# Expert inputs by indirect DMA and transposes in place of one-hot products, with gates applied per slot

## The chip, the cores and the metric

The kernel runs on one core of a Trainium2 chip. The metric is the device time of one execution in microseconds (us); lower is better. Engines are named as the profile names them: PE (TensorE, with PEld for its weight loads), DVE (VectorE), ACT (ScalarE), POOL (GpSimd) and SP (SyncE, which issues the weight loads).

## The reference, cut to what matters

The model has two layers over 512 tokens of 1024 channels. Each layer is a token mixer followed by a mixture of 16 experts, of which each token takes two. All arithmetic is float32.

```python
def grouped_moe(x, router_w, router_b, w1, w3, w2):
    logits = xt @ router_w + router_b
    scores = softmax(logits)
    ...                                   # best of 4 expert groups, then its top 2 experts
    gates = top_w / sum(top_w)
    def expert_block(args):               # rows of the tokens that chose expert e
        xb, e = args
        hb = silu(xb @ w1[e]) * (xb @ w3[e])
        return hb @ w2[e]
    ys = ys * buf_gate[:, None]
    out = segment_sum(ys, buf_tok)        # back to the tokens

h = layer_norm(ALPHA * h + y, ln1_g[l], ln1_b[l])
y = grouped_moe(h, router_w, router_b, moe_w1[l], moe_w3[l], moe_w2[l])
h = layer_norm(ALPHA * h + y, ln2_g[l], ln2_b[l])
```

## The kernel before, in words

A float32 product is made of three passes in a rounded format (`mm3`, L341): each operand is split into a high part (ACT's cast, L337) and a low part (DVE's subtraction, L338), and PE adds high x high, high x low and low x high (L343, L345, L344). Weights come from DRAM in pieces of 1 MB on SP's queue (`load`, L323) into a ring of ten buffers; each piece is split as two halves of 128x1024.

`moe` (L1281) is the stage that the change touches; it runs once in each layer. `route` (L1069) chooses experts and gives each token its rank within its expert (`rke`). Each expert has 96 slots (`CAP`). Experts are taken in groups (`GROUPS`: 0-1, 2-4, 5-7, 8-10, 11-13, 14-15). For a group, `one_hot` (L1185) builds on DVE a matrix `A` of zeros and ones (tokens x slots), and `gather_x` (L1201) multiplies the stored rows by it on PE: for each of 8 channel blocks, the high rows `hi` and the low rows `lo` times `A`, over 4 blocks of tokens, 64 products for a group, 288 columns wide for a group of three experts and 256 for a group of two (L1212). `gathered` (L1216) copies the results from PSUM to the `hx` tiles, high parts on ACT (L1221), low parts on DVE (L1222). The first group is gathered apart, while the last block of tokens is still being normed (L1323).

The loop over `e` (L1330) issues, for each expert: the first product with W1 (48 matmuls), the product with W2 of the expert before (48, `expert_out`, L1260), a share of the gathering for the next group, the product with W3 (48), and `expert_mid` (L1250): silu (ACT, L1256), the product of both halves (DVE, L1257), and a transposition on PE (`transpose_split`, L1224, matmul line L1231) that ACT (L1233) and DVE (L1234) take out of PSUM as high and low parts. `expert_out` copies its result out on ACT (L1278) and writes it to DRAM (`yd`). In iteration 1, `places` (L1122), some fifty small DVE operations, works out where each token finds its two results, and the gates. In iteration 14 `rest` (L1401) transposes `A` of experts 14 and 15, whose results never go to DRAM, and `overflow` (L1452) tests whether any expert has more than 96 tokens; every engine meets at that test.

At the end `collect` (L1418) fetches for each block of tokens the two result rows by indirect DMA from POOL's queue (L1425), scales the first by its gate on ACT (L1429), and adds the second times its gate on DVE (L1433). `combine` (L1502) adds everything in PSUM and norms it.

While layer 0's experts run, POOL also works out the parameters of the next layer's state-space mixer (`s5_params`). Before the experts, `settle` (L1051) norms the rows of each block of tokens and splits them into `hi` and `lo`. The order of the work on each engine is set ahead by a planner, from program order, priorities and the few hints `issue_after`; on the chip each engine then runs its list in order.

Of the kernel before, what the change touches and what calls it, by code (L numbers as in the profile page):

```python
# [19 lines left out]
P = 128  # L20
T = 512
# [12 lines left out]
WIDE = 3 * CAP * 4  # L34
# [25 lines left out]
def shape_constants():  # L60
    c = {}
    p = np.arange(P)
    ident = np.eye(P, dtype=np.float32)
    shut = np.where(p[None, :] >= p[:, None], -1e30, 0.0).astype(np.float32)
    before = (p[:, None] < p[None, :]).astype(np.float32)
    iota = np.broadcast_to(p.astype(np.float32) + 1.0, (P, P))
    misc = np.zeros((P, 64), np.float32)
    misc[:, 0:16] = np.arange(16)
    misc[:, 16:32] = 16 - np.arange(16)
    misc[:, 32:36] = 4 - np.arange(4)  # L70
    misc[:, 36] = -0.5
    misc[:, 37] = 1.0
    misc[:, 40:40 + len(TURNS)] = TURNS
    c["shut"] = np.concatenate([shut, before], 1)
# [45 lines left out]
class Kernel:  # L120
# [8 lines left out]
    def run(self):  # L129
# [7 lines left out]
        self.y_dram = self.dram.tile([(NG + SPILL) * CAP, D], F32, name="yd")  # L137
# [115 lines left out]
    def hx(self, n):  # L253
        return self.keep.tile([P, WIDE], F32R, tag="hx", name="hx", bufs=8)[:, 0:n]
# [696 lines left out]
    def row_loads(self, l):  # L951
# [19 lines left out]
        if l == 0:  # L971
            zr = self.mr.tile([P, 2048], F32, tag="raw", name="zr", bufs=2)[0:CAP, 0:D]
            nc.gpsimd.memset(zr, 0.0)
        yield
# [146 lines left out]

    def places(self, r, pool):  # L1122
        V = self.nc.vector
        t = lambda nm, sh, dt=F32: pool.tile([P] + sh, dt, tag=nm, name=nm, bufs=1)
        ps, M, s = r["ps"], r["M"], r["s"]
        oh, v, wm = t("oh", [128]), t("v", [2, NT]), t("wm", [NT])
# [7 lines left out]
        for j in range(2):  # L1134
            V.tensor_tensor(rk[j], oh[:, j], s, OP.mult)
            V.tensor_reduce(v[:, j], rk[j], AX.X, OP.add)
        gt, den = t("gt", [2, NT]), t("den", [NT])
        V.tensor_tensor(den, v[:, 0], v[:, 1], OP.add)
        V.reciprocal(den, den)
        V.tensor_tensor(gt, v, den[:, None, :].to_broadcast([P, 2, NT]), OP.mult)  # L1140
# [27 lines left out]
        pf, gm0, gl = t("pf", [2, NT]), t("gm0", [2, NT]), t("gl", [2, NT])  # L1168
# [5 lines left out]
        V.tensor_scalar(gm0, gt, float(1.0 / ALPHA), None, OP.mult)  # L1174
        V.tensor_tensor(b2, b2, gm0, OP.mult)
        last = t("glast", [2, NT])
        for x in range(2):
            V.tensor_tensor(gl, b2, oh[:, :, :, NG + x], OP.mult)
            V.tensor_tensor(last[:, x], gl[:, 0], gl[:, 1], OP.add)
            V.tensor_tensor(gm0, gm0, gl, OP.subtract)  # L1180
        V.tensor_scalar(b2, gm0, 0.0, None, OP.is_gt)
        V.tensor_tensor(pos, pf, b2, OP.mult)
        r.update(gm=gm0, pos=pos, exi=exi, mci=mci, cnti=cnti, last=last)

    def one_hot(self, pool, r, group, parts=1):  # L1185
        e, n = group
        w = self.width(n)
# [10 lines left out]
    def width(self, n):  # L1198
        return CAP if n == 3 else P

    def gather_x(self, A, out, ks):  # L1201
        nc = self.nc
        n, w = A.shape[2:]
        for k in ks:
            if n == 3:
                ps = [self.bank(t, "gx")[:, 0:n * w] for t in ("zo", "zz")[k % 2]]
            else:
                b = self.bank("oz"[k % 2], "gx")
                ps = [b[:, 0:n * w], b[:, n * w:]]
            for s, rows in enumerate((self.xh, self.rl)):  # L1210
                for c in range(NT):
                    nc.tensor.matmul(ps[s], rows[c][:, k * P:(k + 1) * P], A[:, c].rearrange("p e s -> p (e s)"),  # L1212
                                     start=c == 0, stop=c == NT - 1)
            self.gathered(ps, out, k, n, w)

# [8 lines left out]
    def transpose_split(self, src, h, lo, tags="oz"):  # L1224
        nc = self.nc
        w = src.shape[0]
        for half in range(2):
            ps = self.bank(tags[half], "tx")[:, 0:4 * w]
            for q in range(4):
# [3 lines left out]
            self.mid = (nc.scalar.copy(h[:, sl], ps).ins,  # L1233
                        nc.vector.tensor_tensor(lo[:, sl], ps, h[:, sl].bitcast(F32), OP.subtract).ins)  # L1234
# [25 lines left out]
    def expert_out(self, pool, w, g, mkload, dst, us=range(4), ps=None, y=None):  # L1260
# [15 lines left out]
        for n in range(2):  # L1276
            ns = slice(n * 512, (n + 1) * 512)
            nc.scalar.copy(y[0:CAP, ns], ps[n])  # L1278
        nc.scalar.dma_start(dst, y[0:CAP])

    def moe(self, l, lg, nb, rs):  # L1281
# [6 lines left out]
        with self.pool("mw") as mw, ExitStack() as spare:  # L1288
# [41 lines left out]
            for e in range(NE):  # L1330
# [6 lines left out]
                at, n = e - GROUPS[g][0], GROUPS[g][1]  # L1337
                if at == 0:
                    cur, nxt = nxt, ([], [])
                w = at * self.width(n)  # L1340
                x = [[t[k // 4][:, k % 4, w:w + CAP] for k in range(KD)] for t in cur]
                with ExitStack() as after:
# [4 lines left out]
                    self.calm = False  # L1347
                if e == NE - 1:
                    half = self.expert_out(mw, W2, pend, mk(e - 1), None, range(2))
                elif pend is not None:  # L1350
                    y13 = self.keep.tile([P, WIDE], F32, tag="hx", name="y", bufs=8)[:, 0:D] if e == NE - 2 else None
                    self.expert_out(mw, W2, pend, mk(e - 1), Y[(e - 1) * CAP:e * CAP, :], y=y13)
                if e < NE - 2:
                    if at == 0:
                        A = self.one_hot(mw, r, GROUPS[g + 1])
                    self.gather_x(A, nxt, range(*((0, 3, 6, 8), (0, 4, 8))[n == 2][at:at + 2]))
# [44 lines left out]
    def rest(self, A, r, mw):  # L1401
# [3 lines left out]
        pg = self.bank("z", "gs")  # L1405
        for x in range(2):
            ps = self.bank("o", "at")
            for c in range(NT):
                nc.tensor.transpose(ps[0:CAP, c * P:(c + 1) * P], A[:, c, x, 0:CAP].bitcast(F32), self.ident)
            nc.scalar.copy(self.at[x], ps[0:CAP])  # L1410
            for c in range(NT):
                nc.tensor.matmul(pg[0:CAP, x:x + 1], A[:, c, x, 0:CAP].bitcast(F32), r["last"][:, x, c:c + 1],
                                 start=c == 0, stop=c == NT - 1)
            gs = self.hi.tile([P, 1], F32, name=f"gs{x}")[0:CAP]
            nc.vector.tensor_copy(gs, pg[0:CAP, x:x + 1])
            self.gs.append(gs)

    def collect(self, r, Y, slots):  # L1418
# [3 lines left out]
        for c in range(NT):  # L1422
# [4 lines left out]
            act, dve = self.cut  # L1427
# [24 lines left out]
    def overflow(self, l, r, mw, Y, wf):  # L1452
# [4 lines left out]
        with tc.If(most > CAP):  # L1457
            A = mw.tile([P, WIDE], F32R, tag="A", name="oA", bufs=1)[:, 0:NT * P].rearrange("p (c s) -> p c s", c=NT)
            sl = mw.tile([P, D], F32, tag="sl", name="osl", bufs=1)
            xh, xl, wt = (self.hx(D) for _ in range(3))  # L1460
            wh, wl = wt[:, 0:T], wt[:, T:]
            rk = self.keep.tile([P, NT], F32, tag="ork", name="ork")
            x = [[t[:, k * P:(k + 1) * P] for k in range(KD)] for t in (xh, xl)]
            for b in range(1, BLOCKS):
                with tc.For_i(0, NE, 1) as e:
                    ce = nc.values_load(r["cnti"][0:1, bass.ds(e, 1)], min_val=0, max_val=T)
                    with tc.If(ce > CAP * b):
# [3 lines left out]
                                        rk[:, :, None].to_broadcast([P, NT, P]), OP.is_equal)  # L1471
                        for k in range(KD):
# [23 lines left out]
                        for n in range(2):  # L1496
                            nc.scalar.copy(sl[:, n * T:(n + 1) * T], product(W2, n))
# [74 lines left out]
```

## Time and profile before

| | us |
|---|---|
| median of 3 runs | 2233.0 (2229.27 to 2236.12) |
| the profiled execution, its own time | 2232.6 |
| its span in the trace | 2230.8 |

| engine | busy, us | share of the span |
|---|---|---|
| PE | 2161.2 | 97% |
| PEld | 1617.5 | 73% |
| DVE | 1554.7 | 70% |
| ACT | 1246.3 | 56% |
| POOL | 437.3 | 20% |

The experts' stage of layer 0 runs from about 505 to 1130 us of the span, that of layer 1 from about 1596 us to the end. A matmul's record lasts longer than the time until the next one starts, since matmuls are pipelined; the cost of one is therefore read as the distance between starts.

### The profile page before, as it was taken

The numbers are of one execution on the slowest core, as the hardware profiler recorded it, in microseconds if no ns is written. First come the engines' busy times: TensorE is split into PE (matmuls) and PEld (weight loads), VectorE is DVE, ScalarE is ACT, GpSimd is POOL, SyncE is SP. The second block draws the span as 40 slices with busy tenths as digits, with TensorE's granted clock in tenths as the row PEclk, the third lists the DMA queues.
The fourth block names the chain that finished last, engine by engine and source line by source line (L and its number), as shares of the span: only waits on it lengthen the run. The fifth ranks groups of instructions, "written<-read, shape, count | busy, mean of one in ns | idle before, by whom it ended". The sixth has DMA issues, their size and how long they took to land. (4 is left out here: it accounts for less than half of the span.)

```text
span 2230.8 us, 28031 instructions
## 1 busy us (share of the span) xinstructions
PE 2161.2 (97%) x10498; PEld 1617.5 (73%) x10501; DVE 1554.7 (70%) x1986; ACT 1246.3 (56%) x1580; POOL 437.3 (20%) x491
## 2 busy tenths in 40 slices
PE   7999999999999999999999999999899999999997
PEld 5678678877777777776676877888677777777765
DVE  8443533458988998887864435334798888888878
ACT  4333123336777777777744322223477777777764
POOL 5310141120039920000250204211300000000003
PEclk9989999999999999999999999999999999999999
DMA  6121275327989999997931313343389999999965
GB/s 193 51 59 45 69 255 191 113 71 281 336 310 351 337 360 355 342 358 281 376 114 38 75 57 128 117 170 130 125 322 355 351 357 351 346 358 360 340 262 197
DMA packets 188171, 517.96 MB, mean 232 GB/s; under 512 B 17968, under 2 KB 71856, under 8 KB 188016
## 3 DMA queue, kind: packets, MB, share of 16 engines
q1 hardware_dynamic: 173312, 476.69, 59.7%
q10 hardware_dynamic: 10960, 25.67, 3.5%
q0 software_dynamic: 3744, 13.63, 1.6%
q8 instruction: 85, 1.39, 0.3%
q14 instruction: 70, 0.57, 0.1%
HBM read 490.13 MB, written 22.81 MB: 230 GB/s over the span
## 5 line engine op out<-in xcount | busy, mean ns | idle before, releaser
L338 DVE TENSOR_TENSOR wl<-raw,wh 128x1024 fp32r<-128x1024 f32 x850 | 1046.1, 1250 | 342.2 <-ACT wh L337 328.6
L337 ACT CAST wh<-raw 128x1024 fp32r<-128x1024 f32 x872 | 907.3, 1051 | 457.9 <-PE e L345 197.8
L344 PE MATMUL e<-wl,hx 128*96 128x512 f32 x1024 | 406.3, 397 | 7.5 <-PEq L1457 6.7
L345 PE MATMUL e<-wh,hx 128*96 128x512 f32 x1024 | 404.0, 395 | 0.0
L343 PE MATMUL e<-wh,hx 128*96 128x512 f32 x1024 | 391.2, 394 | 0.3 <-ACT wh L337 0.3
L343 PE MATMUL pjf<-hx,wh 128*128 128x512 f32 x608 | 245.1, 403 | 4.8 <-DVE v L210 4.8
L345 PE MATMUL pjf<-hx,wl 128*128 128x512 f32 x608 | 244.3, 402 | 2.1 <-DVE wl L338 2.1
L344 PE MATMUL pjf<-hx,wh 128*128 128x512 f32 x608 | 244.9, 403 | 0.8 <-DVE hx L211 0.7
L344 PEld LDWEIGHTS e<-wl,hx 128*96 128x96 f32 x1024 | 165.3, 161 | 75.8 <-DVE wl L338 5.5
L343 PEld LDWEIGHTS e<-wh,hx 128*96 128x96 f32 x1024 | 165.2, 162 | 67.5 <-ACT wh L337 0.7
L345 PEld LDWEIGHTS e<-wh,hx 128*96 128x96 f32 x1024 | 165.9, 162 | 65.8 <-issue 0.5
L344 PE MATMUL e<-wl,gh 128*96 128x512 f32 x512 | 201.3, 393 | 0.2
L345 PE MATMUL e<-wh,gl 128*96 128x512 f32 x512 | 201.3, 393 | 0.0
L1425 POOL DMA_INDIRECT yg<-yd,pos x16 | 28.0, 1751 | 882.0 <-DVE wl L338 586.4
L343 PE MATMUL e<-wh,gh 128*96 128x512 f32 x512 | 195.0, 393 | 0.0
L343 PEld LDWEIGHTS pjf<-hx,wh 128*128 128x128 f32 x608 | 115.6, 190 | 33.9 <-DVE v L210 6.0
L345 PEld LDWEIGHTS pjf<-hx,wl 128*128 128x128 f32 x608 | 115.6, 190 | 29.6 <-DVE wl L338 2.6
L344 PEld LDWEIGHTS pjf<-hx,wh 128*128 128x128 f32 x608 | 115.4, 190 | 29.5 <-DVE hx L211 1.9
L344 PEld LDWEIGHTS e<-wl,gh 128*96 128x96 f32 x512 | 82.7, 161 | 36.3 <-DVE wl L338 2.2
L343 PEld LDWEIGHTS e<-wh,gh 128*96 128x96 f32 x512 | 82.5, 161 | 35.2
L345 PEld LDWEIGHTS e<-wh,gl 128*96 128x96 f32 x512 | 82.5, 161 | 34.3
L1212 PE MATMUL gx<-A,hi 128*128 128x288 f32 (+1 forms) x640 | 97.3, 296 | 0.0
(489 smaller groups left out, 2853.8 us busy)
## 6 DMA issues: line engine op xcount, KB each, us to landing
raw<-in_moe_w_dram SPq DMA_DIRECT2D x384, 1024.0 KB, 6.0
raw<-in_w_in_dram SPq DMA_DIRECT2D x44, 1024.0 KB, 5.2
yd<-y ACTq DMA_DIRECT2D x28, 384.0 KB, 4.8
raw<-in_w_out_dram SPq DMA_DIRECT2D x8, 1024.0 KB, 6.9
yd<-zr ACTq DMA_DIRECT2D x14, 384.0 KB, 6.2
row<-hd POOLq DMA_DIRECT2D x8, 512.0 KB, 7.7
rawu<-in_w_up_c_dram SPq DMA_DIRECT2D x8, 512.0 KB, 3.4
tab<-in_ct_dram ACTq DMA_DIRECT2D x12, 256.0 KB, 2.7
```

The source lines that it names most:

```text
L337: self.cut = (nc.scalar.copy(hv, v).ins, (eng or nc.vector).tensor_tensor(lv, v, hv.bitcast(F32), OP.subtract).ins)
L338: (eng or nc.vector).tensor_tensor(lv, v, hv.bitcast(F32), OP.subtract).ins)
L343: mm(out, lh, rh, start=start, stop=False)
L344: mm(out, lh, rl, start=False, stop=False)
L345: mm(out, ll, rh, start=False, stop=stop)
L1212: nc.tensor.matmul(ps[s], rows[c][:, k * P:(k + 1) * P], A[:, c].rearrange("p e s -> p (e s)"), start=c == 0, stop=c == NT - 1)
L1425: nc.gpsimd.indirect_dma_start(out=yg[j], out_offset=None, in_=Y[:, :], in_offset=bass.IndirectOffsetOnAxis(ap=r["pos"][:, j, c:c + 1], ax ...
```

## The change

`settle` now also writes the normed rows of each block of tokens to a DRAM tensor `x_dram`, from POOL's queue. For experts 2 to 15 (14 of 16), `gather_x` is gone. A new function `slots` builds the one-hot matrix in bfloat16 and multiplies it on PE, for each expert, by a table of only 5 columns (the token's index in two parts, its gate in three), which gives for each slot the row to fetch and its gate. `fetch` then gets the 96 rows of an expert by an indirect DMA from POOL's queue, one expert ahead, and the existing `transpose_split` turns them on PE into channels x slots and splits them. Experts 0 and 1 are gathered as before. `gates`, a new list of small DVE operations in iteration 0, makes the table; `places` loses its operations on gates. `expert_out` scales by the slot's gate as it copies the result out on ACT, so `collect` only adds two rows, the first half of the channels on DVE and the second on POOL. `rest` takes the bfloat16 `A` and no longer computes gates. The `hx` tiles shrink from 1152 to 1024 columns, and one row of zeros at the end of `yd` stands for results that are not in DRAM.

```diff
@@ settle
         self.apply_norm(t, [t[:, 0:512], t[:, 512:1024]], nb, rs, self.gb, adds)
+        nc.gpsimd.dma_start(self.x_dram[c * P:(c + 1) * P, :], t)
@@ new
+    def gates(self, r, pool):
+        ...
+        V.tensor_copy(R[:, :, :, 0], self.misc[:, 56:57, None].to_broadcast([P, NT, NE]))
+        V.tensor_copy(R[:, :, :, 1], self.misc[:, 57:61, None].to_broadcast([P, NT, NE]))
+        V.tensor_tensor(G, r["M"], r["s"], OP.mult)
+        V.tensor_reduce(den, G, AX.X, OP.add)
+        ...
+    def slots(self, pool, r, g):
+        ...
+        A = pool.tile([P, 2 * WIDE], BF16, tag="A", name="As", bufs=1)[:, 0:NT * n * CAP]
+        ...
+        V.tensor_tensor(A, self.iota[:, None, None, 0:CAP].to_broadcast([P, NT, n, CAP]),
+                        r["rke"][:, :, e:e + n, None].to_broadcast([P, NT, n, CAP]), OP.is_equal)
+        ps = self.bank("o", "ix")[0:CAP]
+        for x in range(n):
+            for c in range(NT):
+                nc.tensor.matmul(ps[:, x * COLS:(x + 1) * COLS], A[:, c, x], r["R"][:, c, e + x],
+                                 start=c == 0, stop=c == NT - 1)
+        ...
+        V.tensor_copy(part, p3[:, :, 0])
+        V.tensor_tensor(idx, p3[:, :, 1], part, OP.add)
+        V.tensor_reduce(gate, p3[:, :, 2:], AX.X, OP.add)
+        ...
+    def fetch(self, r, e):
+        t = self.keep.tile([P, D], F32, tag="hx", name="xr", bufs=8)[0:CAP]
+        self.nc.gpsimd.indirect_dma_start(out=t, out_offset=None, in_=self.x_dram[:, :],
+                                          in_offset=bass.IndirectOffsetOnAxis(ap=r["idx"][e], axis=0))
+        return t
@@ expert_out
-            nc.scalar.copy(y[0:CAP, ns], ps[n])
+            nc.scalar.activation(y[0:CAP, ns], ps[n], AF.Copy, scale=gate)
@@ moe, loop over e
+                if 0 < e < NE - 1:
+                    xr = self.fetch(r, e + 1)
                 ...
                     a1 = self.expert_in(W1, x, mk(e), ("pj", "pj"), ready if e == 0 else ())
+                if e == 0:
+                    with tc.issue_after(self.chosen):
+                        self.gates(r, self.hi)
+                        self.slots(mw, r, 0)
                 ...
-                if e < NE - 2:
-                    if at == 0:
-                        A = self.one_hot(mw, r, GROUPS[g + 1])
-                    self.gather_x(A, nxt, range(*((0, 3, 6, 8), (0, 4, 8))[n == 2][at:at + 2]))
+                if at == 0 and e < NE - 2:
+                    A = self.slots(mw, r, g + 1)
+                if 0 < e < NE - 1:
+                    cur = self.transpose_split(xr, self.hx(KD * CAP), self.hx(KD * CAP), "zo", False)
@@ rest
-                nc.tensor.transpose(ps[0:CAP, c * P:(c + 1) * P], A[:, c, x, 0:CAP].bitcast(F32), self.ident)
+                nc.tensor.matmul(ps[0:CAP, c * P:(c + 1) * P], A[:, c, x], self.ident_b, start=True, stop=True)
             ...
-            for c in range(NT):
-                nc.tensor.matmul(pg[0:CAP, x:x + 1], A[:, c, x, 0:CAP].bitcast(F32), r["last"][:, x, c:c + 1],
-                                 start=c == 0, stop=c == NT - 1)
@@ collect
-            with tc.issue_after(act):
-                nc.scalar.activation(yg[0], yg[0], AF.Copy, scale=r["gm"][:, 0, c:c + 1])
-            with tc.issue_after(dve):
-                for i in range(2):
+            with tc.issue_after(self.cut[1]):
+                for i, eng in enumerate((nc.vector, nc.gpsimd)):
                     sl = slice(i * 512, (i + 1) * 512)
-                    nc.vector.scalar_tensor_tensor(yg[0][:, sl], yg[1][:, sl], r["gm"][:, 1, c:c + 1], yg[0][:, sl],
-                                                   OP.mult, OP.add)
+                    eng.tensor_tensor(yg[0][:, sl], yg[1][:, sl], yg[0][:, sl], OP.add)
```

## Rows read from the trace of the kernel before

**Rows 1.** Busy time of each engine by stretch, then clock, DMA share, GB/s.

```profile
530.00:560.00 30.00, 30.00 (x141) 21.30 (x140) 27.26 (x42) 23.03 (x26) 0.00 (x0) 1.00 0.89 316
...
760.00:800.00 40.00, 39.07 (x180) 27.33 (x179) 39.81 (x35) 30.14 (x35) 35.37 (x25) 1.00 0.96 339
...
840.00:880.00 40.00, 40.00 (x193) 28.78 (x191) 34.95 (x35) 30.85 (x37) 0.00 (x0) 1.00 0.97 351
...
1980.00:2020.00 40.00, 40.00 (x186) 28.57 (x185) 36.38 (x35) 31.51 (x36) 0.00 (x0) 1.00 0.99 361
```

**Rows 2.** ACT in time order: silu of experts 1 and 13, layer 0.

```profile
552.79 0.58 ACT L1256 ACTIVATE sl<-e 96x512 f32<-96x512 f32 x1
...
997.90 1.28 ACT L1256 ACTIVATE sl<-e 96x512 f32<-96x512 f32 x2 [1.50 <-PE e L345]
```

**Rows 3.** PE in time order (start, length): gathering products, then the next matmul.

```profile
750.20 1.76 PE L1212 MATMUL gx<-A,hi 128*128 128x288 f32 x12
751.80 0.40 PE L343 MATMUL e<-wh,hx 128*96 128x512 f32 x1
...
955.96 0.28 PE L1212 MATMUL gx<-A,hi 128*128 128x256 f32 x1
956.08 0.39 PE L344 MATMUL e<-wl,hx 128*96 128x512 f32 x1
```

**Rows 4.** PE in time order: four transpositions among an expert's matmuls.

```profile
727.83 0.49 PE L1231 MATMUL tx<-cs,sl 96*128 96x96 f32 x4
728.11 0.45 PE L345 MATMUL e<-wh,hx 128*96 128x512 f32 x1
728.40 0.40 PE L343 MATMUL e<-wh,hx 128*96 128x512 f32 x1
728.63 0.39 PE L344 MATMUL e<-wl,hx 128*96 128x512 f32 x1
```

**Rows 5.** PE in time order: products of one column.

```profile
1035.13 0.76 PE L1412 MATMUL gs<-glast,A 128*96 128x1 f32 x8
1035.75 0.51 PE L1409 MATMUL at<-cs,A 128*96 128x128 f32 x3
```

**Rows 6.** DVE by line and shape: count, busy us, mean ns, idle before.

```profile
L1234 DVE TENSOR_TENSOR gl<-tx,gh 128x384 fp32r<-128x384 f32 x64 | 33.4, 550 | 0.5 <-ACT gh L1233 0.5
L1222 DVE CAST hx<-gx 128x288 fp32r<-128x288 f32 x64 | 28.5, 454 | 12.4 <-PE gx L1212 10.8
...
L1433 DVE SCALAR_TENSOR_TENSOR yg<-yg,gm 128x512 f32<-128x512 f32 x16 | 13.3, 882 | 0.0
...
L1148 DVE TENSOR_TENSOR w<-oh,cn 128x64 f32<-128x64 f32 x4 | 0.9, 219 | 0.0
```

**Rows 7.** SP's waits, 560 to 1020 us (total, times, longest); then DMA issues.

```profile
SPq L323 <- DVE wl L338: 361.1, 133, 10.2
...
raw<-in_moe_w_dram SPq DMA_DIRECT2D x384, 1024.0 KB, 6.0
...
yg<-yd,pos POOLq DMA_INDIRECT x16, 8.3
```

**Rows 8.** Columns as in group 1: a stretch behind the meeting of the engines.

```profile
2160.00:2164.00 4.00, 4.00 (x19) 2.81 (x18) 4.00 (x5) 3.67 (x4) 0.00 (x0) 1.00 1.02 409
```

**Rows 9.** POOL in time order: parameters, first and last of 134; two fetches.

```profile
645.64 1.27 POOL L438 TENSOR_SCALAR pe_xc<-small 128x8 f32<-128x8 f32 x1 [138.25 <-DMA small<-in_small_dram]
...
794.25 1.44 POOL L560 TENSOR_TENSOR small<-r,q 128x128 f32<-128x128 f32 x1
...
1096.42 5.68 POOL L1425 DMA_INDIRECT yg<-yd,pos  x1 [5.11 <-DVE wl L338]
1102.40 0.94 POOL L1425 DMA_INDIRECT yg<-yd,pos  x1 [0.30 <-issue]
```

**Rows 10.** POOL by line and shape: a plain DMA's issue, an addition.

```profile
L976 POOL DMA_DIRECT2D row<-hd x8 | 4.9, 613 | 10.7 <-DVE rwg L963 10.7
...
L944 POOL TENSOR_TENSOR mg<-mg,gsg 128x512 f32<-128x512 f32 x32 | 42.9, 1343 | 210.6 <-DVE gsg L943 198.2 <-ACT warm L997 12.0
```

More of the change, by code (lines that the diff above doesn't have):

```diff
@@ new lines, in slots @@
+    def slots(self, pool, r, g):
+        nc = self.nc
+        V = nc.vector
+        e, n = GROUPS[g]
+        A = pool.tile([P, 2 * WIDE], BF16, tag="A", name="As", bufs=1)[:, 0:NT * n * CAP]
+        A = A.rearrange("p (c e s) -> p c e s", c=NT, e=n)
+        V.tensor_tensor(A, self.iota[:, None, None, 0:CAP].to_broadcast([P, NT, n, CAP]),
[5 more added lines that the diff above has]
+                                 start=c == 0, stop=c == NT - 1)
+        p3 = ps[:, 0:n * COLS].rearrange("p (e w) -> p e w", e=n)
+        idx = self.hi.tile([P, 3], I32, tag="idx", name="idx", bufs=2)[0:CAP, 0:n]
+        gate = self.hi.tile([P, 3], F32, tag="gate", name="gate", bufs=3)[0:CAP, 0:n]
+        part = self.hi.tile([P, 3], F32, tag="part", name="part", bufs=2)[0:CAP, 0:n]
+        V.tensor_copy(part, p3[:, :, 0])
+        V.tensor_tensor(idx, p3[:, :, 1], part, OP.add)
+        V.tensor_reduce(gate, p3[:, :, 2:], AX.X, OP.add)
+        for x in range(n):
+            r["idx"][e + x], r["gate"][e + x] = idx[:, x:x + 1], gate[:, x:x + 1]
+        return A
@@ L1133, in places @@
         rk = [t(nm, [NT, NE]) for nm in ("w0", "w1")]
[L1134 to L1140, printed above, removed]
         cnt = ps[:, 64:80]
@@ L1173, in places @@
         V.tensor_tensor(pf, pf, rs, OP.add)
[L1174 to L1183, printed above, removed]
+        V.scalar_tensor_tensor(b2, es, float(NG), b2, OP.is_ge, OP.mult)
+        V.tensor_scalar(off, pf, -1.0, float(ZERO), OP.mult, OP.add)
+        V.tensor_tensor(off, off, b2, OP.mult)
+        V.tensor_tensor(pos, pf, off, OP.add)
+        r.update(pos=pos, exi=exi, mci=mci, cnti=cnti)
     def one_hot(self, pool, r, group, parts=1):
-        e, n = group
-        w = self.width(n)
+        (e, n), w = group, P
         A = pool.tile([P, WIDE], F32R, tag="A", name="A", bufs=1)[:, 0:NT * n * w]
@@ L1258, in expert_mid, with expert_out @@
         return self.transpose_split(sl, h, lo)
-    def expert_out(self, pool, w, g, mkload, dst, us=range(4), ps=None, y=None):
+    def expert_out(self, pool, w, g, mkload, dst, us=range(4), ps=None, y=None, gate=None):
         nc = self.nc
@@ L1336, in moe @@
                 g = max(i for i, (a, n) in enumerate(GROUPS) if e >= a)
-                at, n = e - GROUPS[g][0], GROUPS[g][1]
-                if at == 0:
-                    cur, nxt = nxt, ([], [])
-                w = at * self.width(n)
-                x = [[t[k // 4][:, k % 4, w:w + CAP] for k in range(KD)] for t in cur]
+                at = e - GROUPS[g][0]
+                if g == 0:
+                    x = [[t[k // 4][:, k % 4, at * P:at * P + CAP] for k in range(KD)] for t in nxt]
+                else:
+                    x = cur
+                if 0 < e < NE - 1:
+                    xr = self.fetch(r, e + 1)
                 with ExitStack() as after:
@@ L1408, in rest @@
             for c in range(NT):
-                nc.tensor.transpose(ps[0:CAP, c * P:(c + 1) * P], A[:, c, x, 0:CAP].bitcast(F32), self.ident)
+                nc.tensor.matmul(ps[0:CAP, c * P:(c + 1) * P], A[:, c, x], self.ident_b, start=True, stop=True)
             nc.scalar.copy(self.at[x], ps[0:CAP])
-            for c in range(NT):
-                nc.tensor.matmul(pg[0:CAP, x:x + 1], A[:, c, x, 0:CAP].bitcast(F32), r["last"][:, x, c:c + 1],
[L1413 to L1416, printed above, removed]
+            self.gs.append(r["gate"][NG + x])
     def collect(self, r, Y, slots):
@@ L1457, in overflow @@
         with tc.If(most > CAP):
-            A = mw.tile([P, WIDE], F32R, tag="A", name="oA", bufs=1)[:, 0:NT * P].rearrange("p (c s) -> p c s", c=NT)
+            At = mw.tile([P, WIDE], F32R, tag="A", name="oA", bufs=1)
+            A = At[:, 0:NT * P].rearrange("p (c s) -> p c s", c=NT)
             sl = mw.tile([P, D], F32, tag="sl", name="osl", bufs=1)
-            xh, xl, wt = (self.hx(D) for _ in range(3))
-            wh, wl = wt[:, 0:T], wt[:, T:]
+            xh, xl = self.hx(D), self.hx(D)
+            wh, wl = At[:, T:2 * T], At[:, 2 * T:]
             rk = self.keep.tile([P, NT], F32, tag="ork", name="ork")
+            gk = self.keep.tile([P, 1], F32, tag="ogk", name="ogk")
             x = [[t[:, k * P:(k + 1) * P] for k in range(KD)] for t in (xh, xl)]
@@ L1471, in overflow @@
                                         rk[:, :, None].to_broadcast([P, NT, P]), OP.is_equal)
+                        V.tensor_copy(rk, r["G"][:, :, bass.ds(e, 1)].rearrange("p c o -> p (c o)"))
+                        pg = self.bank("o", "ogs")
+                        for c in range(NT):
+                            nc.tensor.matmul(pg[:, 0:1], A[:, c].bitcast(F32), rk[:, c:c + 1],
+                                             start=c == 0, stop=c == NT - 1)
+                        V.tensor_copy(gk, pg[:, 0:1])
                         for k in range(KD):
```

64 lines of the change are left out of this document (34 added, 30 removed).

## The prediction

> **What bounds the kernel now.** I read the share of busy time first, then the stretches of the experts' stage, then what single engines do in order of time there, then the waits of the weight queue.
>
> In a steady stretch PE is busy for all of 40 us, while DVE is busy for 34.95, ACT for 30.85, and the DMA engines are shown 0.97 busy at 351 GB/s [rows 1]. So PE is the bound, DVE stands at 87%, and DMA has to be looked at. From expert 1 to expert 13 the silu moves from 552.79 to 997.90 us: 12 periods of 37.1 us [rows 2]. PE's own starts rebuild that period. Twelve gathering products of 288 columns take 1.60 us, 0.133 each [rows 3]; an expert's matmul takes 0.23 [rows 4]; four transpositions delay the matmuls around them by 0.28 and the 0.06 by which the following one is longer, 0.34 together [rows 4]. One expert is 3 x 48 matmuls, two sets of four transpositions, and a third of 64 gathering products: 144 x 0.23 + 0.68 + 2.84 = 36.6 us, half a microsecond short of the period. PE does nothing but this, without gaps; what is taken from its list is taken from the time, as long as nothing else comes up as late.
>
> The weights are no bound yet: SP's queue spent 361.1 of 460 us waiting for DVE to free a buffer, and a load lands 6.0 us after its issue, while ten buffers of a period of 37.1 / 12 = 3.1 us each are 31 us deep [rows 2, 7].
>
> **The change, part by part.** All sums are made against the profiled execution, 2232.6 us; the median of the three runs, 2233.0, is 0.4 higher.
>
> *Gathering removed.* Per layer 4 groups x 64 products of 288 columns and one group x 64 of 256 columns. Over both layers 512 x 0.133 = 68.1 us, and 128 x 0.12 = 15.4 us (955.96 to 956.08) [rows 3]. The gate products of `rest` go too: 2 layers x 16 at 0.62 / 8 = 0.078, 2.5 us [rows 5]; its transpositions stay in another type, taken as equal. Together 86.0 us of PE.
>
> *Transpositions added.* 14 experts x 2 layers x 2 sets of four, the same shape that the kernel has already: 56 x 0.34 = 19.0 us [rows 4].
>
> *Index products added.* 16 experts x 4 x 2 layers = 128 products of five columns in bfloat16. No row shows this form. The nearest, one column in float32, costs 0.078 [rows 5]; I take it, 10.0 us, and keep nothing as the other end. PE's net is 86.0 - 19.0 - 10.0 = 57.0 us, and a period of 37.1 becomes 37.1 - 2.84 + 0.68 + 0.31 = 35.2 us.
>
> *DVE beside it.* Per expert, 8/3 casts of 0.454 go (1.2 us) and two subtractions of 0.550 come (1.1), with three small operations for each group at about 0.22 [rows 6]. Its work per expert stays at 34.95 x 37.1 / 40 = 32.4 us [rows 1, 2], 92% of the new period: hidden, but barely. It isn't hidden in two places. Between 760 and 800 us DVE is busy 39.81 of 40 and PE already loses time (180 matmuls, not 193) while POOL computes the next parameters [rows 1]; there the shorter list of PE buys nothing. POOL's work lasts from 645.64 to 795.7, four periods [rows 9]; none to all of them lose their 1.9 us, and I give back 3 us. In iteration 0, fifteen operations of about 0.22 (`gates`, and the copies of `slots`) and one more comparison are new, some 4 us, where DVE is busy 27.26 of 30 [rows 1, 6], and PE has lost its share of the gathering there, which was the cover; `places` saves about as much one iteration later, where it is less needed. I give back 2 us per layer, 4 in all, between 0 and 8.
>
> *ACT.* Two copies of a set of four replace casts of about the same number; ACT is at 30.85 of 40 [rows 1]. Nothing.
>
> *Writing the rows.* Four issues of 0.613 us on POOL per layer [rows 10]. What stands behind them on POOL is the next block's reciprocal root, for which DVE and the logits wait. POOL waits for DVE before each of those; I take nothing and keep 2 us.
>
> *Fetches.* 28 indirect DMAs. One needs 0.94 to 5.68 us on POOL [rows 9] and lands 8.3 us after issue [rows 7], 14 us at the worst. They are issued at the start of an iteration and PE turns the rows two products later, 96 x 0.23 = 22 us. The cover is 8 us. If it is gone, PE stands still with the next expert's matmuls behind the transposition.
>
> *End of a layer.* DVE's 16 scaled additions of 0.882 [rows 6] become 8 plain ones, and POOL gets 8 of 1.343 [rows 10], four in a row per layer: 5.4 us, in the time in which PE adds four blocks. Only in the last layer is DVE busy without a gap up to the end. I take a gain of 1 us, between a loss of 2 and a gain of 3.
>
> Sum: 57.0 - 3 - 4 + 1 = 51 us, 2232.6 - 51 = 2181.6, and with the 0.4 of the median **2182 us**. With the index products at nothing and no time given back it is 2182 - 10 - 7 - 2 = 2163.
>
> **The rivals.** *DMA becomes the bound.* An expert now moves 12 x 1.049 + 0.39 MB = 12.98 MB (weights by [rows 7], and 96 result rows of 4 KB), and 12.98 MB / 37.1 us is 350 GB/s, as the stretch shows [rows 1]. With the fetched rows it is 13.37 MB in 35.2 us, 380 GB/s. For: the busiest 40 us show a share of 0.99 at 361 GB/s [rows 1]. If that is the ceiling, a period is 13.37 / 0.361 = 37.0 us, and nothing is won: about 2231. If the ceiling lies halfway, at 371, it is 36.0: half, about 2206. Against: 409 GB/s in a stretch in which PE, DVE and ACT work as always [rows 8], and a queue that waits for buffers, not for transfers [rows 7]. The Trainium skill, "SBUF — State Buffer", section "A bandwidth-pool intuition that's wrong (but worth ruling out)", puts the path from HBM to one core at about 358 GB/s; by that page an expert would take 37.3 us, an estimate, and this change would bring nothing. The trace disagrees, with its 409 [rows 8]. I give the full ceiling 0.07, the half one 0.06.
>
> *The fetches stand behind POOL's parameter work, and the kernel is slower.* POOL's 134 rows of parameters run without a break to 795.7 us [rows 9]. Iteration 5 starts where its silu would be, 552.79 + 4 x 37.1 = 701, less 11 us of its first product: 690; the rows of expert 6 are turned at about 712, 704 with the shorter periods. If the planner lists that fetch after the whole chain, it lands at 795.7 + 0.9 + 8.3 = 805, PE stands for 100 us, and the time is about 2282. The kernel gets slower from the point where the fetch lands after 704 + 51 = 755. For: POOL's list is fixed ahead, and POOL is busy 35.37 of 40 us [rows 1]. Against: the fetch precedes most of the chain in the program, and needs nothing that is late. Slower altogether: 0.08. That some fetches of layer 0 come late by 15 to 40 us in all, 2195 to 2222: 0.14.
>
> **How the numbers follow.** The forecast, between 2163 and 2195, has 0.62; the late fetches that leave a gain 0.14; the half ceiling 0.06; gains between these, by DVE's lists at 92%, 0.03; all faster, 0.85. The full ceiling is no change, 0.07, and the long wait slower, 0.08. A measurement of this kernel tells about 0.3%, 7 us, from no change. The range that leaves out no more than 2 in 10 goes from 2163 to the end of the partly late fetches, 2222.
>
> **What would show it.** Right: periods of the silu near 35.2 us, PE busy all of 40 us, no product L1212, 56 sets of transpositions more at 0.34, and 380 GB/s in the steady stretches. Each give-back would be seen as PE idle in iteration 0 and between 640 and 800 us. The DMA rival would show ACT waiting for `raw` from DRAM, and SP no longer waiting for DVE. The POOL rival would show PE waiting at the transposition for a DMA that fills the fetched rows, in experts 6 to 9 of layer 0, with POOL's fetches after its parameter work. The prediction is wrong if the periods shorten and the time doesn't, or if a product of five columns costs several times 0.078.

## The result, and the profile after

The changed kernel takes 2247.2 us (median of 20 runs), the kernel before 2228.4 in the same session: a ratio of 1.0077, 95% interval 1.0058 to 1.0096. It is slower, where a gain of 51 us was forecast. The profiled execution of the changed kernel lasts 2255.2 us (span 2253.4), that of before 2232.6 (span 2230.8): 22.6 us to account for. The single executions of the changed kernel lie between 2234.6 and 2262.8, so the profiled one is 8 us above their median; below, ratios are taken from medians and the places of the time from profiles.

Busy time by stretch of the changed kernel (the columns of [rows 1]): two stretches of layer 0, then one from the first and one from the second half of layer 1's experts.

```profile
680.00:720.00 40.00, 16.44 (x84) 11.62 (x82) 18.54 (x18) 14.81 (x17) 38.43 (x68) 0.76 0.60 218
720.00:760.00 40.00, 25.80 (x114) 18.34 (x115) 20.14 (x23) 17.77 (x20) 12.64 (x20) 0.77 0.53 189
...
1760.00:1800.00 40.00, 40.00 (x190) 28.39 (x189) 36.58 (x35) 33.34 (x39) 1.81 (x2) 1.00 1.00 379
...
1960.00:2000.00 40.00, 39.08 (x180) 26.89 (x178) 34.39 (x35) 31.59 (x39) 2.50 (x2) 1.00 0.96 372
```

The third row is what was forecast: PE without a gap, 379 GB/s. The first two hold a hole in which PE works 42 of 80 us. In the fourth PE loses a microsecond in 40. The silu of experts 5 and 6 in layer 0 (ACT in time order, answering to [rows 2]) give the size of the hole:

```profile
684.47 0.58 ACT L1283 ACTIVATE sl<-e 96x512 f32<-96x512 f32 x1
...
759.53 0.59 ACT L1283 ACTIVATE sl<-e 96x512 f32<-96x512 f32 x1
```

75.06 us between two experts, where a period is 35. What PE waited for in the whole execution (us in total, times, longest):

```profile
PE tx L1256 <- DMA xr<-xd,idx: 37.8, 1, 37.8
...
PE e L348 <- PEq L1480: 11.3, 2, 5.8
PE e L349 <- DVE wl L343: 11.3, 26, 0.6
PE cmb L1543 <- POOL yg L1457: 8.8, 2, 5.4
```

One wait of 37.8 us at the transposition for a fetch; two at the branch around the block for more than 96 tokens (L1480); 26 small ones for VectorE's splits; two for the sums of gathered rows. POOL in time order shows the first and the last of these: fetch of expert 5, start of layer 1's parameter work, two of its operations, fetch of expert 6; then, at the end of the layer, an addition and the gather behind it.

```profile
597.69 2.17 POOL L1174 DMA_INDIRECT xr<-xd,idx  x1 [32.64 <-PE tx L1256]
637.87 0.28 POOL L443 TENSOR_SCALAR pe_xc<-small 128x8 f32<-128x8 f32 x1 [38.02 <-DMA small<-in_small_dram]
...
671.59 1.21 POOL L437 TENSOR_SCALAR pe_r<-pe_k 128x64 f32<-128x64 f32 x1
...
701.20 0.37 POOL L437 TENSOR_SCALAR pe_p<-pe_p 128x64 f32<-128x64 f32 x1
...
730.03 1.02 POOL L1174 DMA_INDIRECT xr<-xd,idx  x1 [0.16 <-issue]
...
1112.42 7.30 POOL L1457 TENSOR_TENSOR yg<-yg 128x512 f32<-128x512 f32 x1 [5.24 <-DMA yg<-yd,pos]
1119.87 0.96 POOL L1452 DMA_INDIRECT yg<-yd,pos  x1 [0.15 <-issue]
```

The fetch of expert 6 stands behind the parameter work, which began at 637.87; it is issued at 730.03. Counted from the silu of expert 15 (1075.62 before, 1092.69 after), all eight gathers of layer 0's end had left POOL after 32.8 us before, and have after 41.0 now: the third stands behind an addition that waits 5.24 us for a landing and then takes 7.30 us itself.

Where the 22.6 us are, by the silu and by PE's own marks in both profiles (after minus before):

| from, to | before | after | difference |
|---|---|---|---|
| up to expert 1, both layers | | | -10.1 |
| expert 1 to 13 without the hole (layer 0: 465.98 - 39.9) | 445.1 + 443.0 | 426.1 + 425.9 | -36.1 |
| the hole, 75.06 in place of the 35.17 of the first run below | | | +39.9 |
| expert 13 to 15, around the branch | 77.7 + 78.0 | 81.6 + 80.5 | +6.4 |
| expert 15 to its last product, layer 0 | 41.8 | 49.5 | +7.7 |
| from there to expert 0 of layer 1 | 501.2 | 512.8 | +11.6 |
| expert 15 of layer 1 to the end | 65.4 | 68.5 | +3.2 |

The +11.6 goes with TensorE's clock: over the way from expert 15 to expert 0 of layer 1 the rows of 10 us, each (1 - granted clock) x 10, add up to 8.5 us before and 27.3 after, which more than covers it. Three rows of the mixer of the changed kernel are at the lower level (0.50, 1.2 GHz), with PE shown busy and VectorE, ACT and POOL below 4 us of 10:

```profile
1230.00:1240.00 10.00, 10.00 (x39) 6.00 (x36) 2.04 (x3) 2.66 (x7) 0.13 (x2) 0.50 0.01 2
1240.00:1250.00 10.00, 10.00 (x42) 5.66 (x41) 2.77 (x7) 3.17 (x7) 0.10 (x1) 0.50 0.00 0
1250.00:1260.00 10.00, 10.00 (x33) 4.96 (x31) 2.91 (x6) 3.20 (x7) 0.13 (x2) 0.50 0.00 0
```

### The profile page after: what moved, and what is told of

Its sections match the earlier page's. It is cut to its first block, busy times and chain, and to the rows that moved or that the text cites. A ratio compares the mean times of both kernels' runs of the same rounds, so it can differ in the third digit from the quotient of the medians.

```text
span 2253.4 us, 27509 instructions
## 1 busy us (share of the span) xinstructions
PE 2120.9 (94%) x10180; PEld 1564.4 (69%) x10181; DVE 1532.0 (68%) x1986; ACT 1229.7 (55%) x1548; POOL 445.4 (20%) x535
## 5 line engine op out<-in xcount | busy, mean ns | idle before, releaser
L343 DVE TENSOR_TENSOR wl<-raw,wh 128x1024 fp32r<-128x1024 f32 x850 | 1026.6, 1242 | 392.0 <-ACT wh L342 366.8
L342 ACT CAST wh<-raw 128x1024 fp32r<-128x1024 f32 x872 | 895.8, 1050 | 426.3 <-PE e L350 150.1
L348 PE MATMUL e<-wh,gh 128*96 128x512 f32 x512 | 180.2, 394 | 0.0
L1174 POOL DMA_INDIRECT xr<-xd,idx x28 | 43.2, 1543 | 675.5 <-PE tx L1256 498.4
L350 PEld LDWEIGHTS e<-wh,gl 128*96 128x96 f32 x512 | 82.5, 161 | 36.2 <-DVE gl L1259 3.5
L949 POOL TENSOR_TENSOR mg<-mg,gsg 128x512 f32<-128x512 f32 x32 | 42.8, 1342 | 212.2 <-DVE gsg L948 187.9
```

Source lines behind the costliest of these rows:

```text
L342: self.cut = (nc.scalar.copy(hv, v).ins, (eng or nc.vector).tensor_tensor(lv, v, hv.bitcast(F32), OP.subtract).ins)
L343: (eng or nc.vector).tensor_tensor(lv, v, hv.bitcast(F32), OP.subtract).ins)
L348: mm(out, lh, rh, start=start, stop=False)
L350: mm(out, ll, rh, start=False, stop=stop)
L949: nc.gpsimd.tensor_tensor(mg[m], mg[m], sg, OP.add)
L1174: self.nc.gpsimd.indirect_dma_start(out=t, out_offset=None, in_=self.x_dram[:, :], in_offset=bass.IndirectOffsetOnAxis(ap=r["idx"][e], axi ...
```

## The experiments

The theory after the result: the gain of PE's shorter list is there (periods of 34.8 us up to expert 7), and is lost in four places that have nothing to do with it: the order on POOL around the parameter work, the order on POOL at the end of a layer, the branch, and something that makes the periods from expert 7 on 36.15 us. The rival for the hole: VectorE, at 92%, would have stopped PE there anyway.

**The parameter work in nine pieces, each behind a fetch.** The generator of the parameters gets other points at which it yields, and

```diff
-                    with tc.issue_after(self.mid[0]), tc.issue_after(self.mid[1]):
+                    with tc.issue_after(self.mid[0]), tc.issue_after(self.mid[1]), tc.issue_after(self.fetched):
                         done = next(prep, 0) == 0
```

where `self.fetched` is the fetch that was issued last.

> The parameter work of layer 1 is cut into nine shorter pieces, and each piece stands on POOL behind the fetch that was issued last, so that a fetch follows each piece. Theory (the fetch of expert 6 stood behind about 100 POOL instructions): the step from expert 5 to expert 6 in layer 0 falls from 75 us to 35 us, PE's wait of 37.8 us at the transposition is gone, and the time is 37 to 43 us under the changed kernel's 2247, about 2207. Rival (VectorE, at 92% of the period and slowed by POOL, would have held PE up in that stretch anyway): the one wait is replaced by many short waits of PE for VectorE's splits, and the gain is 15 to 25 us, about 2227.

2223.4 us; ratio 0.9976 (0.9957 to 0.9996) where the changed kernel had 1.0077, so 1.0% or 22 us less. POOL and then ACT of this run in time order:

```profile
661.40 2.05 POOL L1180 DMA_INDIRECT xr<-xd,idx  x1 [0.16 <-issue]
...
693.24 2.03 POOL L1180 DMA_INDIRECT xr<-xd,idx  x1 [0.17 <-issue]
```

```profile
684.73 0.59 ACT L1290 ACTIVATE sl<-e 96x512 f32<-96x512 f32 x1
...
719.90 0.59 ACT L1290 ACTIVATE sl<-e 96x512 f32<-96x512 f32 x1
```

The fetch of expert 6 leaves at 661.40, and the step from expert 5 to 6 is 35.17 us. PE waits 0.2 us for VectorE between 640 and 760 us. So the hole was the order on POOL, 39.9 us of it, and VectorE doesn't take its place. By the time alone the rival would have won (22 us, its 15 to 25). The span fell by 32.7, since other places gave 7 us back, and the median by less still, since the profiled execution of the changed kernel lies 8 us above its median. Expert 9 to 10 takes 38.4 us in place of 36.0, and the way from the last product of expert 15 in layer 0 to the first transposed projection of layer 1 (PE's first product into the tile `pjt`) takes 71.4 us in place of 50.8, of which 7.5 are only the last product's coming earlier. The next runs take that up.

**The sums on VectorE alone.** POOL issues the gathers and adds nothing:

```diff
-                for i, eng in enumerate((nc.vector, nc.gpsimd)):
+                for i in range(2):
                     sl = slice(i * 512, (i + 1) * 512)
-                    eng.tensor_tensor(yg[0][:, sl], yg[1][:, sl], yg[0][:, sl], OP.add)
+                    nc.vector.tensor_tensor(yg[0][:, sl], yg[1][:, sl], yg[0][:, sl], OP.add)
```

> Both halves of each sum of gathered rows go to VectorE; POOL only issues the eight gathers. Theory (POOL's adds, which wait for a landing, hold back the gathers behind them): PE's wait for the sums (5.4 us in layer 0, 3.4 us in layer 1) shrinks below 2 us, the last gather is issued some 15 to 25 us earlier, and the time falls by 6 to 9 us, to about 2239. If the 30 us at half clock in the next mixer (1230 to 1260) come from that pause of PE, another 10 to 15 us go, to about 2226. Rival (VectorE now stands at the landing and holds back its last splits for PE): no change or up to 5 us slower.

2243.8 us; ratio 1.0052 (1.0034 to 1.0071), 0.25% or 5.6 us less than the changed kernel's. The two intervals overlap, so the medians alone don't show it; the profile does. PE's wait for the sums, 8.8 us, is no longer among its waits of 2.2 us and more; expert 15 has its last product after 42.0 us (49.5 with POOL's additions, 41.8 before), and `combine` its last after 54.5 (60.5, 54.3); the last gather starts 32.1 us behind the silu of expert 15 in place of 40.0, 8 us earlier where 15 to 25 were expected; and layer 1 ends 64.7 us after its expert 15, not 68.5. The clock in the mixer that follows still costs 20.4 us, so this wait of PE alone was not what lowered it.

**Both.**

> The paced parameter work and the sums on VectorE together. If the two are separate causes the gains add: 43 to 55 us under 2247, 2192 to 2204, which is under the kernel before (2228) too. If the hole only hid another limit: not under 2215.

2217.2 us, ratio 0.9943 (0.9922 to 0.9964): faster than the kernel before, and 30 us under the changed kernel, about what the two edits gave singly (22 and 5.6). Of the expected 43 to 55, 13 us are missing. The way to the first transposed projection takes 64.8 us here and 71.4 in the paced run, where the kernel before takes 52.5. Half of that is in one row each of PE, DVE and POOL in time order, where layer 1 begins:

```profile
1128.40 0.80 PE L349 MATMUL pjf<-hx,wh 128*128 128x512 f32 x1 [5.95 <-DVE hx L216]
```

```profile
1121.46 7.49 DVE L216 TENSOR_TENSOR hx<-v,hx 128x512 fp32r<-128x512 f32 x2
...
1130.31 1.28 DVE L216 TENSOR_TENSOR hx<-v,hx 128x512 fp32r<-128x512 f32 x2
```

```profile
1121.47 0.32 POOL L629 TENSOR_TENSOR ei<-ei,Et 128x64 f32<-128x64 f32 x1
1121.75 0.41 POOL L624 TENSOR_TENSOR er<-er,s5c 128x128 f32<-128x128 f32 x1
...
1127.08 0.72 POOL L629 TENSOR_TENSOR ei<-ei,Et 128x256 f32<-128x256 f32 x1
```

Two subtractions that take 1.28 us a pair take 7.49 while POOL runs the S5 tables of layer 1 (powers that its state-space mixer needs) without a break, and PE stands for 5.95. In the kernel before and in the changed kernel the tables begin a little later against the tiles (before: at 1136.71, after VectorE's first pair of them), and no pair there takes more than 1.64 us.

**Both, without the branch.** The line `self.overflow(...)` is left out: the block for experts with more than 96 tokens, which never runs with these inputs, and the branch around it.

> As the run with both edits, without the block for experts of more than 96 tokens and the branch around it (that part of the computation is left out; with these inputs the branch is never taken). Theory (the branch costs PE 5.5 and 5.8 us of standing and the clock's fall behind it some 3 to 5 us more in each layer): 14 to 20 us under the run with both. Rival (the wait is for data that would be late anyway): under 5 us.

2198.0 us, ratio 0.9863 (0.9839 to 0.9888): 19 us less than with it. From expert 13 to 15 layer 0 takes 71.1 us in place of 81.6, so a branch costs 10.4 us there. PE is idle for 7.8 us of that stretch with the branch and for 1.2 without it. The rest goes with the granted clock, which is 1.00 in every row of 10 us from expert 0 to 15 without the branch. With it, in the changed kernel (columns as above):

```profile
1066.00:1070.00 4.00, 0.00 (x0) 0.00 (x0) 0.00 (x0) 0.00 (x0) 0.00 (x0) 0.93 1.03 402
1070.00:1074.00 4.00, 2.54 (x6) 1.80 (x7) 2.45 (x2) 1.99 (x2) 0.00 (x0) 0.50 1.03 420
1074.00:1078.00 4.00, 4.00 (x14) 2.68 (x13) 2.45 (x2) 2.49 (x5) 0.00 (x0) 0.69 1.03 396
```

All engines stand, and when PE works again it is at the lower level at first.

**The tables behind VectorE's tiles.** A copy of one column on POOL reads the last tile, and the tables stand behind that copy:

```diff
+            self.shown = nc.gpsimd.tensor_copy(seen, hh[1][KD - 1][:, 0:1].bitcast(F32)).ins
...
-            after.enter_context(self.tc.issue_after(self.cut[1]))
+            after.enter_context(self.tc.issue_after(self.shown or self.cut[1]))
```

> As the run with both edits (2217), and the S5 tables of layer 1 on POOL stand behind one POOL instruction that waits for the last of VectorE's input tiles. Theory (the tables start 8 us before those tiles are done, and VectorE's half of a tile takes 6.9 us beside them in place of 0.7): the way from the last product of expert 15 to the first transposed projection of layer 1 falls from 64.8 us to 52 to 55 us, as it is in the kernel before, and the time falls by 9 to 13 us to about 2206. Rival (the tables are then late for the mixer, or VectorE is slow there for another reason): within 4 us of 2217, or slower.

2202.3 us, ratio 0.9869 (0.9848 to 0.9889), 0.74% under the run with both edits. The pair of subtractions is back at 1.28 us and PE's wait is gone. The way to the first transposed projection is 59.8 us in this profile, though, not 52 to 55: PE transposes the finished rows 19.7 us after its last product, not 14.5, since it waits 4.0 us for VectorE there and the granted clock is 0.77 and 0.55 in the two rows of 5 us from 1105 to 1115. In the profiles of the four runs below that have the same order there the way takes 54.5, 59.2, 52.4 and 54.2 us, so the forecast of 52 to 55 holds in three of five. The span fell by 3.4 us only, the median by 15; the profiled execution is the slowest of its five (2211.6), so the rest of that gain isn't located.

**The branch at expert 3.** `self.overflow(...)` is called in iteration 3 with a scratch tile of its own, not in iteration 14.

> As the run with the tables behind, and the block for experts of more than 96 tokens, with its branch, stands at expert 3 in place of expert 14. Theory (the branch costs 10.4 us a layer at expert 14 because no finished splits are in stock there; up to expert 7 there is stock): at expert 3 it costs 3 to 5 us a layer, and the time falls by 10 to 15 us against that run. Rival (the standing is the branch's own, wherever it is): the cost moves along, and the time is within 3 us.

2198.9 us, ratio 0.9861 (0.9835 to 0.9887): the same. Expert 13 to 15 takes 71.0 us, and expert 2 to 4 takes 78.3 where the run before had 69.5: the branch costs 8.8 us there, with finished splits in stock (VectorE ahead of PE), not 3 to 5. The theory that the stock decides is wrong; the cost moves along.

**No result rows of experts 2 to 12.** From here to the split on POOL the branch is back at expert 14, and the comparison is with the run with the tables behind the tiles. The write in `expert_out` is left out for these, and their rows are set to zero once.

> As the run with the tables behind, but the results of experts 2 to 12 are not written to DRAM (that part of the output is left out; their rows are filled with zeros once, ahead of layer 0's experts), which takes 0.39 MB of 13.4 MB off each period. If the transfers set the periods of 36.15 us from expert 7 to 13, these fall to 35.0 to 35.3 us, 12 us in all. If VectorE or the order of the instructions sets them, they stay at 36.0 to 36.2 us, and the time is within 3 us.

2212.7 us, ratio 0.9912 (0.9885 to 0.9939). Layer 1's second half, columns as above:

```profile
1960.00:2000.00 40.00, 38.78 (x183) 26.84 (x182) 33.87 (x38) 30.80 (x36) 1.84 (x2) 1.00 0.95 356
```

With 3% fewer bytes the periods of layer 1 are 35.9 to 36.7 us, on average 0.3 longer than with them; those of layer 0 grow too. Transfers don't set them. Why the run is slower at all stays open; its expert 0 of layer 0 already starts 6 us later, behind the added zeros.

**One split of 24 on POOL.** `split_half` gets POOL for the sixth weight block of W3.

> As the run with the tables behind, with one of each expert's 24 subtractions of a split on POOL in place of VectorE (experts 9 to 12 of layer 0, 1 to 12 of layer 1), which takes 1.2 us of VectorE's 32 off a period. If VectorE sets the periods of 36.15 us from expert 7 to 13, they fall to 35.0 us there, 7 us in layer 1 and 4 us in layer 0. If not, they stay, and the time is within 3 us; if POOL's 2.5 us beside VectorE slow it by as much as they take off, they grow, by up to 5 us in all.

2224.1 us, ratio 0.9957 (0.9939 to 0.9974), 22 us slower than without.

```profile
1960.00:2000.00 40.00, 38.78 (x181) 26.81 (x180) 34.39 (x33) 30.17 (x36) 4.52 (x2) 1.00 0.96 362
```

POOL needs 2.63 us on average for its split, VectorE is no less busy, and the periods grow to 36.2 to 37.0 us; one of layer 0 takes 47.2, in which PE waits 3.8 us for POOL's split. This run doesn't clear VectorE by itself, since POOL slows it; but neither less to transfer nor a split less on VectorE shortens the periods.

What remained was the order. In the changed kernel the second half's periods look like this, ACT, DVE and PE in time order:

```profile
1994.11 0.48 ACT L1258 CAST hx<-tx 128x384 fp32r<-128x384 f32 x1 [2.31 <-PE tx L1256]
...
1998.09 5.99 ACT L342 CAST wh<-raw 128x1024 fp32r<-128x1024 f32 x6
...
2008.10 1.26 ACT L1305 ACTIVATE y<-e,gate 96x512 f32<-96x512 f32 x2 [1.26 <-PE e L350]
```

```profile
1995.57 2.36 DVE L343 TENSOR_TENSOR wl<-raw,wh 128x1024 fp32r<-128x1024 f32 x2 [1.49 <-ACT wh L342]
...
1999.17 9.17 DVE L343 TENSOR_TENSOR wl<-raw,wh 128x1024 fp32r<-128x1024 f32 x8 [0.30 <-ACT wh L342]
2010.89 3.49 DVE L343 TENSOR_TENSOR wl<-raw,wh 128x1024 fp32r<-128x1024 f32 x3 [2.56 <-ACT wh L342]
```

```profile
2000.45 0.47 PE L349 MATMUL e<-wl,gh 128*96 128x512 f32 x1 [0.47 <-DVE wl L343]
...
2012.17 0.48 PE L349 MATMUL e<-wl,hx 128*96 128x512 f32 x1 [0.42 <-DVE wl L343]
```

ACT's copy of the new transposition stands ahead of casts and waits 2.31 us for PE. VectorE, which needs the casts, has nothing to do for 1.49 us, and PE catches up with it at 2000.45. VectorE then empties a queue of eight splits, while ACT waits for the last product with W2 to copy the results; VectorE has nothing to do for 2.56 us, and PE catches up again at 2012.17. Up to expert 7 PE transposes behind W2's products, and the planner listed ACT's copies behind the result copies, with casts in between.

**Transpositions behind W2's products, their copies behind the result copies.**

```diff
+                    with ExitStack() as behind:
+                        if e > 1 and e != 3:
+                            behind.enter_context(tc.issue_after(self.last_mm))
+                            behind.enter_context(tc.issue_after(self.y_copy))
                         cur = self.transpose_split(xr, self.hx(KD * CAP), self.hx(KD * CAP), "zo", False)
```

> As the run with the branch at expert 3, and each expert's transpositions stand behind the W2 products of the expert before on PE, and their copies behind that expert's result copies on ACT. In the periods from expert 7 to 13 (36.1 us) the copies stand ahead of eight casts on ACT, ACT waits 2.3 us there, VectorE runs dry for 2.6 us, and PE then waits twice for 0.6 us. Theory (that order sets these periods, neither the transfers nor VectorE's work): they fall to 34.8 to 35.2 us, 6 us in each layer, and the time falls by 9 to 13 us, to about 2188. Rival (the planner moved the casts as well, so PE waits elsewhere): the periods stay at 36.0 us and the time within 3 us.

2181.4 us, ratio 0.9793 (0.9766 to 0.9820). This one stands on the run with the branch at expert 3, and by the ratios it is 15 us under that run, more than the 9 to 13 expected. The silu of experts 9 to 11 of layer 1, and a stretch (columns as above):

```profile
1899.90 1.08 ACT L1296 ACTIVATE sl<-e 96x512 f32<-96x512 f32 x2 [1.24 <-PE e L350]
...
1934.34 1.08 ACT L1296 ACTIVATE sl<-e 96x512 f32<-96x512 f32 x2 [1.24 <-PE e L350]
...
1969.23 1.08 ACT L1296 ACTIVATE sl<-e 96x512 f32<-96x512 f32 x2 [1.37 <-PE e L350]
```

```profile
1920.00:1960.00 40.00, 40.00 (x189) 28.45 (x188) 36.23 (x37) 30.84 (x36) 0.90 (x1) 1.00 0.99 384
```

Most periods are now 34.4 us, PE is busy for all of 40, and its waits for VectorE's splits of expert weights have left the list, with VectorE's work as it was. From expert 7 to 13 the two layers take 419.0 us where the run with the branch at expert 3 took 435.8. This is the fastest version, 2.1% under the kernel before, and it computes all that the changed kernel computes.

**The kernel before, without the branch.**

> The kernel before without the block for experts of more than 96 tokens and the branch around it (that part of the computation is left out; with these inputs the branch is never taken). From expert 13 to 15 the kernel before takes 77.7 us, two of its periods are 73.5 us: if the branch costs there what the trace shows, 4 us a layer, this run is 7 to 10 us under the kernel before. If the branch costs as much as in the changed kernel (10.4 us a layer) and the rest is hidden in the lead of VectorE, it is 18 to 22 us under it.

2226.4 us, ratio 0.9982 (0.9961 to 1.0003). Expert 13 to 15 takes 72.9 us in place of 77.7: the branch costs 4.8 us a layer in the kernel before, less than half of the 10.4 in the changed one. The span fell by 10.7 us as that asks; the medians can't tell it from no change. PE is idle for 3.9 us of that stretch with the branch and for 0.4 without it, and the clock falls less than in the changed kernel. The lowest row of 4 us behind the branch of the kernel before (layer 0) is:

```profile
1056.00:1060.00 4.00, 4.00 (x14) 2.62 (x13) 2.75 (x4) 2.17 (x3) 0.00 (x0) 0.66 0.90 328
```

The profile has a second use: its mixer is the one of the kernel before, and yet the rows of 10 us give 17.0 us of clock from expert 15 to expert 0 of layer 1, against 8.5.

## Why the prediction was wrong

*What held.* PE as the bound, and its list. The 56 sets of transpositions are there; a stretch of PE in the changed kernel has twelve index products in 0.52 us, 0.043 each against the 0.078 taken, so at that price the net of PE's list was some 61 us rather than 57. The forecast period of 35.2 is 34.8 up to expert 7, and 34.4 in the repaired kernel, whose 2181 us lie on the forecast 2182. That agreement is for another kernel than the one forecast: four further edits (paced parameter work, sums on VectorE, tables behind the tiles, copies behind the results), and a branch that moved.

*The step that failed first: fetches.* It set one fetch (5.68 us on POOL, 8.3 to land) against 22 us of PE and found a cover of 8. A fetch took 1.5 us on average. What it missed is that the cover has to be counted from the moment when POOL reaches the fetch, and POOL had 92 us of parameter work in front of it. The rows were on the table [rows 9], and the text named the case as its second rival with the mark by which to know it; the wait of 37.8 us in expert 6 is that mark. What came is that rival's full form, which was put at a wait of 100 us: 126 instructions of the chain, all but its last ten, stand ahead of the fetch. That the size came out within the 15 to 40 us of the milder form is luck. This part of the chain took 92 us, where it took 138 in the kernel before: its instructions took 1.00 us on average up to 699.6, but 0.47 behind it, when VectorE stood with PE. Wrong was the weight: "the fetch precedes most of the chain in the program" was taken as a reason against, though nothing ties POOL's order to that of the program. The paced run shows the price, 39.9 us. The point from which that rival makes the kernel slower was put at a delay of 51 us, because it used the whole forecast gain; with the other losses 17 us of delay would have been enough (39.9 - 22.6).

*End of a layer.* The forecast was a gain of 1 us, and a loss of 2 at worst: it measured a loss of 7.7 in layer 0 and 3.2 in layer 1. The step priced POOL's additions at 1.343 each as work, 5.4 for four, where the four of layer 0 took 11.9, and forgot the rule that it had used elsewhere: what stands behind a waiting instruction waits too. The additions wait for landings, and the gathers stand behind them. With the sums on VectorE alone expert 15 has its last product after 42.0 us again (41.8 before).

*The period.* VectorE at 92% was called hidden but barely; the second half lost 1.3 us a period against the first, and some 12 us in both layers against the forecast 35.2. VectorE's work was not the cause, since the repaired kernel has 34.4 with the same work, and neither were the transfers: 3% fewer bytes shortened nothing. It was the order: the transpositions ahead of W2's products on PE, and their copies ahead of casts on ACT, the engine to which the forecast gave nothing because of its share. The run moved both, so which of the two counts is not shown.

*Not in the sum at all.* The branch (6.4 us more from expert 13 to 15) and the clock of the mixer. Removing the branch and moving it shows its price, 10.4 and 8.8 us against 4.8 before. It doubled in two parts: from expert 13 to 15 PE is idle for 7.9 us in place of 3.9 (layer 0), and (1 - granted clock) x time adds up to 5.1 us in layer 0 and 3.4 in layer 1 in place of 1.7. Why the engines stand longer stays open. A clue only: while the engines stand, the DMA engines run at 382 GB/s in the changed kernel (1064 to 1071) and at 111 before (1051 to 1054); whether the code behind the branch waits for weights is not shown. The clock's +11.6 us is in the one profile of the changed kernel; the kernel before shows 8.5 and, without its branch, 17.0 us of such loss in the same mixer, the repaired kernel 8.5, the other runs 11.9 to 27.4. So it varies from execution to execution. The mean granted clock of whole executions is 0.961 to 0.972 in the 20 of the changed kernel, 0.973 to 0.979 in the 8 with both edits and 0.975 to 0.987 in 57 of the kernel before: part of the loss comes with the change, as the hole and the branch show, but how much of the mixer's does is open.

*The DMA rival.* Refuted: 379 GB/s at a period of 34.7, 384 in the repaired kernel. The Trainium skill, "Perfetto Trace Analysis", section "Engine Utilization" with its "Roofline", gives 358 GB/s as a core's share when both cores of a pair load, and about 435 as the bound of 16 DMA engines for one core alone. The trace agrees: the 379 and 384 lie between the two.

## What to carry to other kernels

Shortening the bound engine's list pays only as far as the new operations have a place in the order of the others: ask of each new transfer what stands ahead of it on the queue that issues it, and of each new wait what stands behind it. An engine that is idle on average (POOL, 1.8 of 40 us in a steady stretch here) is not idle at the moment that matters (38.4 of 40 in the hole), and a copy that waits on a half-empty ACT starves the engine behind it. When the gain is missing, look for it in single long waits first, then in the periods, and only then in shares of busy time.

## What the runs showed of the hardware

POOL and VectorE hold each other up, and which of them pays depends on the moment. Of two POOL operations of one line and shape (128x64), one took 1.21 us at 671.59, where VectorE splits almost without a pause, and the other 0.37 at 701.20, where VectorE stands. The other way round, a dozen of POOL's operations in a row (1121.75 to 1127.8) held one pair of VectorE's subtractions for 7.49 us in place of 1.28. The Trainium skill, "SBUF — State Buffer", section "Who interferes with whom", has a VectorE instruction with two inputs in SBUF contend with POOL's reads of SBUF, and makes the order of issue decide who is kept out. The first observation agrees with it; the second goes further, as a single pair waited through many of POOL's instructions. Beside the same tables in the kernel before a pair lost at most 0.36 us, so POOL's share of the time alone doesn't tell the price.

An indirect DMA's time on POOL ranged from 0.90 to 2.54 us for 96 rows of 4 KB, and to 8.72 us for gathers of 128 rows, all in one execution.
